# First norms of a two-layer decoder trunk: three due times in a schedule of steps

## The chip, the cores and the metric

The kernel runs on one core of one Trainium2 chip. The metric is the device time of one execution in microseconds (us), and the number that counts is the median over several runs. The engines of the core are called PE (the matrix engine), DVE (the vector engine), ACT (the scalar engine), POOL (GpSimd) and SP (which here issues the DMA transfers).

## The reference

The reference is one inference step of a decoder trunk with two layers, run for a prompt of 1024 tokens and a group of 8 sample tokens, model width 1024. Each layer is an RMS norm, a token mixer (HGRN2 in layer 0, a chunked gated MLP in layer 1), a residual add, and a per-layer embedding that is gated from the residual. Only the beginning matters here: two products that don't depend on each other, the first norm and the first projection.

```python
def rmsnorm(x, g):
    xf = x.astype(jnp.float32)
    y = xf * lax.rsqrt(jnp.mean(xf * xf, axis=-1, keepdims=True) + EPS)
    return (y * g.astype(jnp.float32)).astype(x.dtype)
...
        hn = rmsnorm(h, norm_mix[i])
...
    proj = h @ w_in
...
        h = h + gate * (p[i] @ w_ple_proj[i])
```

## The kernel before

Activations lie with the model width on the partitions (8 tiles of 128, `KT`) and the tokens along the free dimension. The 1032 tokens are cut into three chunks of 384, 384 and 264 columns (`W`, `CH`). Every float32 product is made of three matmuls of a reduced float type (`mm3`, L217 to L221): each operand is split into a high and a low part, and high times high, high times low and low times high are summed in PSUM. So every operand goes through a cast on ACT and a subtraction on DVE or POOL: `split_weights` (L146, L147) for weights, `split` (L214, L215) for activations.

PE's instructions keep the order in which the program issues them. The order on the other engines is chosen when the kernel is compiled, by a scheduler that looks at what is ready, at the program's order and at `high_priority`; on the chip each engine then works through its list strictly in turn. `issue_after(x)` pins what it encloses behind the instruction `x` in the list of x's engine.

The program mixes side work into PE's main stream with a clock of steps, the class `Ticks` (L47). A process (a Python generator) is spawned, and each `yield n` lets it sleep for n steps; `tick()` advances the clock by one and runs what is due, in the order of spawning. A step here is only a place in the program's order, not a time.

The opening is arranged like this. `pple` (L327) makes 12 groups of 6 matmuls, the product of p and half of `w_ple_proj`: 4 groups for chunk 0 (groups 0 to 3), 4 for chunk 1 (4 to 7), 4 for chunk 2 (8 to 11). Each group fills one of three PSUM banks (tag `mm`), which ACT empties (`pple_t`, L338) and SP stores. A `tick()` follows every group. Then come, for each chunk c in turn, `fk(c)` and `qq(c)`, the first two tiles of the projection: 24 matmuls each (`proj`, L298, the same three banks), with one `tick()` in the middle and one at the end. Their weights are the transfers `wstg<-in_wina`; the split of the first is issued during the fill, pinned behind the copy of group 8, and that of the second when `take` fetches the pair ahead of `fk(0)`.

For each chunk a process `first_norm(c)` (L440) runs beside this, with four parts:

- the squares: ACT squares the input tiles `xs` in four instructions (L448), each followed by one add (L449) on DVE for chunk 0 and on POOL for chunks 1 and 2. For chunk 1 the squares are pinned behind the latest `pple_t` copy issued so far, for chunk 2 behind the fourth of the eight casts of a norm (`split4`);
- the sum (`norm_sum`, L257): 24 matmuls of one column against a column of ones (`pss`, L269), then the small add `rms_e` on DVE (L272) and the power -0.5 on POOL (`rsq`, L228), all three with priority;
- the broadcast (`norm_bc`, L275): 6 matmuls that spread `rsq` over the partitions (`pbc`, L280);
- the norm proper, issued with the broadcast: for each of 8 tiles one multiply on DVE (`tmp`, L293), one cast on ACT (`bh`, L214) and one subtraction (`bl`, L215), in turn on POOL and DVE. `fk(c)` and `qq(c)` read `bh` and `bl`.

Where they fall is set by two tables: `SQD` is the step at which a chunk's squares start, and `SDEL[c] = (a, b)` puts the sum a steps behind the squares and the broadcast b steps behind the sum.

```python
SQD = (0, 6, 12)
SDEL = ((6, 3), (6, 2), (4, 2))
...
        yield d[0]
        with tc.high_priority(offset=PRI):
            rs = norm_sum(sp, ssq, c)
        yield d[1]
        pbc = norm_bc(rs, c)
```

Of the kernel before, what the change touches and what calls it, by code (L numbers as in the profile page):

```python
# [31 lines left out]
NWARM = 12  # L32
ZQ = 5
FDEL = ((2, 2), (2, 2), (1, 3))
SQD = (0, 6, 12)
OD = (4, 4)
DL = 4
KB = 1
SDEL = ((6, 3), (6, 2), (4, 2))
NDEL = (((1, 2), (1, 3), (2, 2)), ((2, 2), (2, 4), (3, 3)))  # L40
OFF = (0, 384, 768)
W = (384, 384, 264)
# [38 lines left out]
def trunk_kernel(ctx, tc, xT, st, pT, nrm, wina, lbl, gna, wouta, winb, lng, lnb, lngr, lnbr,  # L81
# [129 lines left out]
    last, rest = {}, {}  # L211

    def split(hi, lo, src, eng=V):
        last["split"] = A.copy(hi, src)  # L214
        last["lo"] = eng.tensor_tensor(lo, src, hi.bitcast(F32), ALU.subtract)  # L215
# [41 lines left out]
    def norm_sum(sp, ssq, c):  # L257

        cols = NT[c] + (c == 2)
        pss = pp.tile([P, 512], F32, name="pss", tag="po", bufs=1)  # L260
        parts = ssq if isinstance(ssq, list) else [ssq]

        if c == 2 and "sq" in rest:
            parts = parts + [rest.pop("sq")]

        for i in range(cols):
            o = min(i * P, W[c] - P)
            for j, t in enumerate(parts):
                PE.matmul(pss[:, i:i + 1], t[:, o:o + P], ones[:, 0:1],  # L269
                          start=j == 0, stop=j == len(parts) - 1)  # L270
        e = sp.tile([P, 3], F32, name="rms_e", bufs=2)
        V.tensor_scalar(e, pss[:, :3], D * EPS, None, ALU.add)  # L272
        return rsqrt(sp, e, 3)

    def norm_bc(y, c):  # L275

        pbc = p2[0].tile([P, 512], F32, name="pbc", tag="p2", bufs=2)
        for i in range(NT[c] + (c == 2)):
            n = min(P, W[c] - i * P)
            PE.matmul(pbc[:, i * P:i * P + n], y[:, i:i + 1].broadcast_to([P, P]), ident[:, P - n:], start=True, stop=True)  # L280
        return pbc

    def norm_proc(sp, ssq, src, gi, hh, hl, c, d):
# [6 lines that stand above are left out]
        w = W[c]  # L290
        for j in range(KT):
            t = sp.tile([P, 384], F32, name="tmp", bufs=4)
            V.scalar_tensor_tensor(t[:, :w], src(j), g32[:, gi, j:j + 1], pbc[:, :w], ALU.mult, ALU.mult)  # L293
            split(hh[:, j, :], hl[:, j, :], t[:, :w], V if j % 2 else G)
            if j == 3:
                last["split4"] = last["split"]

    def proj(wt, xh, xl, c):  # L298

# [140 lines left out]
    def first_norm(c):  # L440
        if c:
            yield SQD[c]
        sq = sp.tile([P, KT, 384], F32, name="sq0", bufs=2)[:, :, :W[c]]
        eng = V if c == 0 else G
        for j in range(0, KT, 2):

            with tc.issue_after(last["pple" if c == 1 else "split4"].ins) if c else ExitStack():
                A.activation(sq[:, j:j + 2, :], xs[c][:, j:j + 2, :], AF.Square)  # L448
            eng.tensor_tensor(sq[:, j, :], sq[:, j, :], sq[:, j + 1, :], ALU.add)  # L449
        yield from norm_proc(sp, [sq[:, j, :] for j in range(0, KT, 2)], lambda j: xs[c][:, j, :], 0, hh[c], hl[c], c, SDEL[c])  # L450

# [34 lines left out]
    for c in CH:  # L486
        tk.spawn(first_norm(c))
# [461 lines left out]
    def norm_spawn(c, ssq, gi, act, d):  # L949
        tk.spawn(norm_proc(sp, ssq[c], lambda j: hr[c][j], gi, act[0][c], act[1][c], c, d[c]))  # L950
# [455 lines left out]
```

## Time and profile before

| | before |
|---|---|
| median of 3 runs | 1919.65 us (1918.82 to 1920.35) |
| the profiled execution's own time | 1921.39 us |
| span of the profile, first to last instruction | 1919.7 us |
| PE busy | 1883.1 us (98% of the span) |
| DVE, ACT, POOL busy | 1156.6, 799.9, 433.4 us |
| mean granted clock of PE | 0.991 of full speed |

The span is what the profiler saw between the first and the last instruction. The time of the same execution is 1.69 us more, for what lies around it, and that execution was 1.74 us slower than the median. A matmul row shows PE busy until a modelled end, so the distance between the starts of neighbouring matmuls tells the pace better than their durations. Where an engine sat idle ahead of an instruction, the row gives the idle time and what ended it in square brackets.

### The profile page before, as it was taken

To read this page: it belongs to the slowest core of one execution; us is meant where nothing else is said; L and a number is where in the kernel's file an instruction comes from. 1 tells how busy PE (TensorE), PEld (TensorE's weight loads), DVE (VectorE), ACT (ScalarE), POOL (GpSimd) and SP (SyncE) were. 2 spreads that over 40 slices of the span, in tenths; PEclk is the share of its full clock that TensorE was granted. 3 is DMA by queue.
4 is the path that set the end of the run, shared out by engine and by line. 5 is a ranking of instruction groups with operands and counts; after the bars stand their busy time and mean duration, and the time that the engine had idled before them with its cause. 6 is when DMAs were issued, how large, how long until landed. Compare 5 with 4: busy or idle time off the path is not lost.

```text
span 1919.7 us, 33670 instructions
## 1 busy us (share of the span) xinstructions
PE 1883.1 (98%) x13250; PEld 1856.4 (97%) x13250; DVE 1156.6 (60%) x2600; ACT 799.9 (42%) x1701; POOL 433.4 (23%) x441
## 2 busy tenths in 40 slices
PE   9999999999999998999999999999999998999997
PEld 8999999999999998999999999999999998999997
DVE  5967676766767676411465755587777766311455
ACT  6453544444454546311244544434434345211342
POOL 4110000000010001011233332344445441011321
PEclk8999999999999999999999999999999998999998
DMA  6232323222231326711243343323323237611123
GB/s 213 75 109 69 116 73 102 78 80 78 92 100 59 111 65 189 256 47 53 73 146 116 109 148 96 93 76 118 125 100 107 100 107 216 197 45 45 67 89 111
DMA packets 123886, 203.75 MB, mean 106 GB/s; under 512 B 11408, under 2 KB 96592, under 8 KB 122704
## 3 DMA queue, kind: packets, MB, share of 16 engines
q1 hardware_dynamic: 123728, 201.61, 32.5%
q8 instruction: 104, 1.70, 0.4%
q14 instruction: 54, 0.44, 0.1%
HBM read 148.75 MB, written 52.82 MB: 105 GB/s over the span
## 4 chain that ended last, share of the span: by engine, by line
PE 90%; DVE 5%; DMA 3%; ACT 1%; issue 1%; POOL 1%; SPq 0%; DVEq 0%; ACTq 0%; POOLq 0%
PE ps_proj L219 18%; PE ps_proj L221 18%; PE ps_proj L220 18%; PE ps_o L219 6%; PE ps_o L220 6%; PE ps_o L221 6%; PE ps_d L221 2%; PE ps_d L219 2%; PE ps_d L220 2%; PE psp L1228 1%; PE pt_o L703 1%; PE pC L658 1%; PE pss L269 1%; PE p L624 1%; DMA vb<-vd 1%
## 5 line engine op out<-in xcount | busy, mean ns | idle before, releaser
L219 PE MATMUL ps_proj<-bh,whi 128*128 128x384 f32 (+1 forms) x2160 | 695.2, 322 | 2.3 <-ACT pple_t L338 1.6
L221 PE MATMUL ps_proj<-bh,wlo 128*128 128x384 f32 (+1 forms) x2160 | 680.0, 315 | 0.6 <-DVE wlo L147 0.5
L220 PE MATMUL ps_proj<-bl,whi 128*128 128x384 f32 (+1 forms) x2160 | 678.9, 314 | 1.2 <-POOL bl L215 1.2
L219 PEld LDWEIGHTS ps_proj<-bh,whi 128*128 128x128 f32 x2160 | 407.5, 189 | 3.8 <-ACT pple_t L338 1.7
L220 PEld LDWEIGHTS ps_proj<-bl,whi 128*128 128x128 f32 x2160 | 407.8, 189 | 2.3 <-POOL bl L215 2.3
L221 PEld LDWEIGHTS ps_proj<-bh,wlo 128*128 128x128 f32 x2160 | 406.6, 188 | 1.8 <-DVE wlo L147 1.8
L147 DVE TENSOR_TENSOR wlo<-wstg,whi 128x1024 fp32r<-128x1024 f32 x148 | 186.2, 1258 | 140.6 <-ACT whi L146 139.8
L146 ACT CAST whi<-wstg 128x1024 fp32r<-128x1024 f32 x148 | 155.1, 1048 | 160.2 <-PE ps_proj L220 105.8
L255 POOL TENSOR_TENSOR ssq<-ssq,tmp 128x384 f32<-128x384 f32 (+1 forms) x72 | 76.1, 1057 | 413.1 <-ACT tmp L254 366.3
L884 DVE TENSOR_TENSOR h<-h,ps_o 128x384 f32<-128x384 f32 (+1 forms) x48 | 24.6, 512 | 193.1 <-PE ps_o L221 192.8
L254 ACT ACTIVATE tmp<-h 128x384 f32<-128x384 f32 (+1 forms) x72 | 35.3, 490 | 219.2 <-DVE h L884 168.9
L219 PE MATMUL ps_o<-bh,whi 128*128 128x384 f32 (+1 forms) x384 | 122.1, 318 | 0.0
L220 PE MATMUL ps_o<-bl,whi 128*128 128x384 f32 (+1 forms) x384 | 121.8, 317 | 0.0
L221 PE MATMUL ps_o<-bh,wlo 128*128 128x384 f32 (+1 forms) x384 | 121.8, 317 | 0.0
L146 ACT CAST shi<-ssum 128x512 fp32r<-128x512 f32 x88 | 54.6, 621 | 109.1 <-PE ps_proj L220 59.2
L219 PE MATMUL ps_o<-zh,whi 128*128 128x384 f32 (+1 forms) x288 | 90.1, 313 | 0.0
L221 PE MATMUL ps_o<-zh,wlo 128*128 128x384 f32 (+1 forms) x288 | 89.8, 312 | 0.0
L220 PE MATMUL ps_o<-zl,whi 128*128 128x384 f32 (+1 forms) x288 | 89.7, 312 | 0.0
L215 POOL TENSOR_TENSOR ql<-q,qh 128x384 fp32r<-128x384 f32 (+1 forms) x24 | 22.3, 928 | 254.0 <-ACT qh L214 254.0
L147 DVE TENSOR_TENSOR slo<-ssum,shi 128x512 fp32r<-128x512 f32 x88 | 68.9, 784 | 11.9 <-ACT shi L146 11.9
L661 DVE TENSOR_TENSOR q<-q,t 128x192 f32<-128x192 f32 (+1 forms) x144 | 47.1, 328 | 45.1 <-PE pC L658 38.7
L220 PEld LDWEIGHTS ps_o<-bl,whi 128*128 128x128 f32 x384 | 72.2, 188 | 0.0
(291 smaller groups left out, 3928.8 us busy)
## 6 DMA issues: line engine op xcount, KB each, us to landing
wstg<-in_wina SPq DMA_DIRECT2D x48, 512.0 KB, 3.7
wstg<-in_winb SPq DMA_DIRECT2D x48, 512.0 KB, 3.9
zstg<-ozd SPq DMA_DIRECT2D x22, 384.0 KB, 4.3
pj<-ppd SPq DMA_DIRECT2D x16, 516.0 KB, 4.5
S<-in_st SPq DMA_DIRECT2D x16, 512.0 KB, 5.4
vb<-vd SPq DMA_DIRECT2D x16, 512.0 KB, 4.4
out_so_s<-S SPq DMA_DIRECT2D x16, 512.0 KB, 3.5
wstg<-in_wouta SPq DMA_DIRECT2D x16, 512.0 KB, 3.5
```

Source lines behind the costliest of these rows:

```text
L146: A.copy(hi, src)
L147: V.tensor_tensor(lo, src, hi.bitcast(F32), ALU.subtract)
L215: last["lo"] = eng.tensor_tensor(lo, src, hi.bitcast(F32), ALU.subtract)
L219: PE.matmul(ps, wh, xh, start=first, stop=False, skip_group_check=more)
L220: PE.matmul(ps, wh, xl, start=False, stop=False, skip_group_check=more)
L221: PE.matmul(ps, wl, xh, start=False, stop=last, skip_group_check=more)
L254: A.activation(sq[:, :w], src, AF.Square)
L255: eng.tensor_tensor(ssq, ssq, sq[:, :w], ALU.add)
L269: PE.matmul(pss[:, i:i + 1], t[:, o:o + P], ones[:, 0:1], start=j == 0, stop=j == len(parts) - 1)
L624: PE.matmul(blk(p0, i), blk(Y, i), blk(X, i), start=True, stop=True)
L661: V.tensor_tensor(ql[:, :, 1, :], ql[:, :, 1, :], t2[:, :, 0:1].broadcast_to([P, n, lv]), ALU.mult)
L884: V.tensor_tensor(hr[c][m], hr[c][m], ps[:, :W[c]], ALU.add)
```

## The change

The steps are worked out from the tables and the order of the ticks; the first tick precedes group 0, so step n is the tick behind group n-2.

| chunk | part | before | after |
|---|---|---|---|
| 0 | sum | behind group 5 | the same |
| 0 | broadcast and norm | behind group 8 | behind group 6 |
| 1 | squares | behind group 5 | behind group 3 |
| 1 | sum | behind group 11 | behind group 9 |
| 1 | broadcast and norm | behind `fk(0)` | behind group 11, ahead of `fk(0)` |
| 2 | squares | behind group 11 | the same |
| 2 | sum | behind `qq(0)` | in the middle of `qq(0)` |
| 2 | broadcast and norm | behind `fk(1)` | in the middle of `fk(1)` |

The squares of chunk 1 stay pinned behind the latest copy, which is now that of group 3 and was that of group 5. As the broadcast of chunk 1 now comes ahead of the squares of chunk 2 in the same step, `split4` is kept for each chunk, and chunk 2's squares stay pinned behind chunk 0's fourth cast.

```diff
-SQD = (0, 6, 12)
+SQD = (0, 4, 12)
-SDEL = ((6, 3), (6, 2), (4, 2))
+SDEL = ((6, 1), (6, 2), (3, 2))
...
             if j == 3:
-                last["split4"] = last["split"]
+                last["split4", c] = last["split"]
...
-            with tc.issue_after(last["pple" if c == 1 else "split4"].ins) if c else ExitStack():
+            with tc.issue_after(last["pple" if c == 1 else ("split4", 0)].ins) if c else ExitStack():
```

## Rows read from the trace of the kernel before

**Rows 1.** The page: busy time, share of the span and instructions of each engine.

```profile
PE 1883.1 (98%) x13250; PEld 1856.4 (97%) x13250; DVE 1156.6 (60%) x2600; ACT 799.9 (42%) x1701; POOL 433.4 (23%) x441
```

**Rows 2.** PE's longest wait from 20 us to the end: total us, times, longest.

```profile
PE ps_pple L219 <- ACT h L338: 8.6, 1, 8.6
```

**Rows 3.** Timeline of PE in the opening: start us, us, what.

```profile
15.12 2.73 PE L269 MATMUL pss<-ones,sq 128*128 128x1 f32 x24
17.71 0.42 PE L219 MATMUL ps_pple<-ph,whi 128*128 128x384 f32 x1
...
21.32 0.41 PE L219 MATMUL ps_pple<-ph,whi 128*128 128x264 f32 x1
...
22.76 0.37 PE L219 MATMUL ps_pple<-ph,whi 128*128 128x264 f32 x1
...
25.04 2.73 PE L269 MATMUL pss<-ones,sq 128*128 128x1 f32 x24
29.38 0.69 PE L219 MATMUL ps_proj<-bh,whi 128*128 128x384 f32 x1 [1.61 <-ACT pple_t L338]
...
36.34 0.83 PE L280 MATMUL pbc<-ident,rsq 128*128 128x128 f32 x6
36.92 0.42 PE L219 MATMUL ps_proj<-bh,whi 128*128 128x384 f32 x1
...
41.20 2.73 PE L269 MATMUL pss<-ones,sq 128*128 128x1 f32 x24
43.79 0.42 PE L219 MATMUL ps_proj<-bh,whi 128*128 128x384 f32 x1
```

**Rows 4.** Stretches of the opening: us, engines' busy us (instructions), granted clock, DMA share, GB/s.

```profile
18.00:22.00 4.00, 4.00 (x17) 4.00 (x16) 0.05 (x1) 1.66 (x4) 2.82 (x3) 0.57 1.07 364
...
30.00:36.00 6.00, 6.00 (x23) 6.00 (x22) 4.74 (x7) 5.45 (x9) 5.21 (x6) 0.56 0.50 155
...
42.00:50.00 8.00, 8.00 (x54) 7.52 (x54) 4.58 (x9) 3.19 (x8) 3.13 (x3) 1.00 0.01 2
```

**Rows 5.** Timeline of ACT in the opening.

```profile
15.69 0.85 ACT L448 ACTIVATE sq<-xs 128x768 f32<-128x768 f32 x1
19.64 0.48 ACT L338 COPY pple_t<-ps_pple 128x384 f32<-128x384 f32 x1 [3.10 <-PE ps_pple L221]
20.01 0.85 ACT L448 ACTIVATE sq<-xs 128x768 f32<-128x768 f32 x1
...
28.53 0.51 ACT L214 CAST bh<-tmp 128x384 fp32r<-128x384 f32 x1 [1.92 <-DVE tmp L293]
28.95 0.93 ACT L338 COPY pple_t<-ps_pple 128x264 f32<-128x264 f32 x3
```

**Rows 6.** Timeline of DVE in the opening.

```profile
27.81 0.16 DVE L272 TENSOR_SCALAR rms_e<-pss 128x3 f32<-128x3 f32 x1 [1.53 <-PE pss L269]
27.89 0.61 DVE L293 SCALAR_TENSOR_TENSOR tmp<-xs,g,pbc 128x384 f32<-128x384 f32 x1
...
33.49 0.75 DVE L215 TENSOR_TENSOR bl<-tmp,bh 128x384 fp32r<-128x384 f32 x1 [0.53 <-ACT bh L214]
34.97 1.67 DVE L147 TENSOR_TENSOR wlo<-wstg,whi 128x1024 fp32r<-128x1024 f32 x1 [0.73 <-ACT whi L146]
```

**Rows 7.** Timeline of POOL in the opening.

```profile
18.13 0.85 POOL L228 TENSOR_TENSOR rsq<-rms_e,mhalf 128x3 f32<-128x3 f32 x1 [17.62 <-DVE rms_e L272]
...
22.86 2.03 POOL L449 TENSOR_TENSOR sq<-sq 128x384 f32<-128x384 f32 x2 [0.92 <-ACT sq L448]
...
33.79 1.77 POOL L449 TENSOR_TENSOR sq<-sq 128x264 f32<-128x264 f32 x2
```

**Rows 8.** The third load of chunk 1's input, issued at 12.26 us: us to landing.

```profile
DMA to landing us min/median/max: 4.8/4.8/4.8
```

**Rows 9.** Groups by line and shape, 8 to 58 us: count, then busy us, mean ns.

```profile
L293 DVE SCALAR_TENSOR_TENSOR tmp<-xs,g,pbc 128x384 f32<-128x384 f32 x16 | 8.9, 606 | 5.6 <-PE pbc L280 5.6
...
L215 DVE TENSOR_TENSOR bl<-tmp,bh 128x384 fp32r<-128x384 f32 x8 | 7.5, 937 | 0.5 <-ACT bh L214 0.5
```

## The prediction

> **What bounds the kernel now.** The page comes first: PE is busy for 98% of the span, every other engine for 60% or less [rows 1], so a saving counts only where it takes away idle time of PE or time that PE spends at half clock. The list of PE's waits comes next: after the opening its longest single wait is 8.6 us, in the fill of the last output phase, which the change doesn't touch [rows 2]. What the change moves lies before 60 us, so I read PE's timeline there, row by row [rows 3], and then the granted clock of the same stretch [rows 4].
>
> Two losses stand in it. Ahead of `fk(0)` PE sits idle for 1.61 us [rows 3]. And twice the clock falls to the lower of its levels, 1.2 instead of 2.4 GHz: the granted clock is 0.57 from 18 to 22 us and 0.56 from 30 to 36 us [rows 4]. The full pace is that of `qq(0)`: 24 matmuls from 36.92 to 41.20 us, 0.178 us each [rows 3]. `fk(0)` has 24 matmuls of the same shape and takes 6.96 us, so the second slow stretch costs 6.96 - 4.28 = 2.68 us. Groups 6 and 7, twelve such matmuls, take 3.61 us instead of 2.14, so the first costs 1.47 us [rows 3]. Each stretch follows a sum of 24 one-column matmuls, which takes 2.59 us (17.71 - 15.12, 43.79 - 41.20) [rows 3].
>
> The timelines of the other engines tell why PE waited. `fk(0)` needs a PSUM bank that ACT has to empty; ACT's copies at 28.95 us stand behind a cast that waited 1.92 us for DVE [rows 5]; and DVE's list had `rms_e` of chunk 1 in front, which waited 1.53 us for the sum to end at about 27.6 us [rows 6]. So a sum with no work behind it that PE could do held up DVE, through DVE ACT, and through ACT PE.
>
> **The change, part by part.** No arithmetic and no transfer is added or removed, and no SP instruction moves in the program; only places in the order change.
>
> *Chunk 0's broadcast, behind group 6 instead of 8.* Group 6 ends halfway through the 3.61 us of groups 6 and 7, at 19.5 us. `rsq` ended at 18.13 + 0.85 = 18.98 us [rows 7], so the broadcast need not wait, unless one of chunk 1's adds stands ahead of it on POOL, 1.0 us each [rows 7]. It costs 0.58 us at either place (36.34 to 36.92 us) [rows 3], and up to twice that at half clock. Chunk 0's multiplies can then begin 2.7 us sooner (it began at 22.76 - 0.58 = 22.18 us).
>
> *Chunk 1's squares, two groups sooner.* They cost nothing new: ACT stood idle for 3.10 us between the first square and the copy of group 6, with the other three squares behind that copy [rows 5]. The inputs must have landed: the third load was issued at 12.26 us and took 4.8 us, so it was there at 17.1 us [rows 8].
>
> *Chunk 1's sum, behind group 9 instead of 11.* A group of chunk 2 takes (25.04 - 22.76) / 3 = 0.76 us [rows 3], so PE reaches the sum at 25.04 - 1.52 = 23.5 us, and the sum ends at 26.1. The adds ended at 22.86 + 2.03 = 24.89 us [rows 7], barely in time before; now they must come 1.4 us sooner. Groups 10 and 11 and the broadcast, 1.52 + 0.58 us, then lie between the sum and `fk(0)`, and cover the chain of DVE and ACT. That is worth the wait, 1.61 us, at most and nothing at least.
>
> *The clock after that sum.* The slow stretch behind it cost 2.68 us. Its row shows a sum and then a gap. In the new order matmuls follow the sum at once, as they did after the first sum, which left a loss of 1.47 us, and after the third, which left none: 42 to 50 us has a granted clock of 1.00 [rows 4]. So the gain is 2.68 - 1.47 = 1.21 us or 2.68. I take 1.21, because the first sum is the one that stands, as this one will, among the groups of the fill. Nothing in the rows excludes a longer slow stretch, which is one of the rivals. Together the two terms give 2.82 to 4.29 us.
>
> A rule of the Trainium skill (TensorE: Matmul & The Clock Gate, section on HAM oscillation) makes PE's idle gaps what sends the clock back to half. By that alone the second stretch would go with its gap and the sum would be 4.29; the row of the first sum, with no gap ahead of the fall, speaks against leaning on it.
>
> *What is late next.* With PE sooner, DVE's chain for chunk 0 may set the pace. Its last subtraction ended at 34.24 us and the low half of the second weights at 36.64 [rows 6]; `qq(0)` uses that in its third matmul, at 36.92 + 0.36 = 37.28 us, so there was 0.64 us to spare. If DVE keeps its order, with `rms_e` ahead of the fifth multiply, the chain moves by 1.52 us with the sum, and `qq(0)` can start at 36.64 - 1.52 - 0.36 = 34.76 us, a gain of 2.16. If the fifth multiply goes ahead of `rms_e`, it can move by up to the 2.7 us of the broadcast, a gain of 3.34. So this caps the gain between 2.16 and 3.34 us. The two bounds meet around 2.8 us, which I take.
>
> *Chunk 2's sum and broadcast, one step sooner.* The adds ended at 33.79 + 1.77 = 35.56 us, and PE came to the sum at 41.20 [rows 3, 7]. It comes half a projection (2.14 us) and the gain sooner, at some 36.3 us, while the adds, pinned behind chunk 0's fourth cast, move forward too. Nothing, while that cover of 0.7 us or more holds; without it PE waits for what is missing, 1 us at the worst.
>
> *Afterwards.* The rows show no resource other than PE with a fixed time behind the opening, so I let the gain carry through whole. It is a difference within the profiled execution (1921.39 us, of which 1919.7 are span); I take it from the median: 1919.65 - 2.8 = **1916.85 us**. What a measurement of this kernel can tell from no change is about 0.2%, 3.84 us; so this forecast counts as the same.
>
> **The rivals.** *The sum waits for its adds.* If ACT's list keeps the remaining squares behind the copies of groups 6 to 8, as now (the second square ran right behind the copy of group 6 [rows 5]), the adds end at 24.9 us or later, PE idles 1.4 us ahead of the sum, and the sum ends at 27.5. Groups 10, 11 and the broadcast bring `fk(0)` to 29.6 us. With a slow stretch of 1.47 to 2.68 us behind it, `qq(0)` starts at 35.4 to 36.6, a gain of 0.3 to 1.5: **1918.7 us** in the middle. For it: the order of ACT is made at compile time, and the loads bound it. Against: the pin is two copies looser.
>
> *The clock stays up.* As after the third sum, no fall: 1.61 + 2.68 = 4.29 us, **1915.4 us**, if DVE's list also changes enough to feed it. For it: the granted clock of 1.00 [rows 4]. Against: the first sum. It is also what the skill's rule on gaps would give.
>
> *The second weights come too late: slower.* Chunk 1's norm is now issued ahead of the fetch of the second weights; before, it was issued behind it. If DVE therefore does chunk 1's steps ahead of `wlo` (L147), `qq(0)` stalls. They cost 8 x 0.606 + 4 x 0.937 = 8.6 us of DVE [rows 9]; all ahead would put the start of `qq(0)` at 34.76 + 8.6 = 43.4 us, 6.4 us later than before: **1926 us**. It decides from 2.2 us of steps ahead, about three multiplies; half of them would give 1921.8. Against: the second weights were split in the gaps of this list before, with DVE idle for 0.73 us ahead of them [rows 6].
>
> **How the numbers follow.** The forecast has 0.43, the clock that stays up 0.25, the sum that waits 0.22, the late weights 0.10. The range goes from 1914.8 (4.29 us and half of the first slow stretch, whose matmuls move against the sum) to 1920.0 (the waiting sum with nothing gained, plus the scatter of the runs); above it lie most of the late weights. Faster by over 0.2% needs 3.84 us: most of the clock that stays up, and a little of the forecast, 0.27. Slower by over 0.2% is the late weights with over half of the steps ahead, 0.05. The rest, 0.68, is the same.
>
> **What would show it.** Right: no wait of PE ahead of `fk(0)`; groups 10 and 11 between the second sum and the broadcast without a gap; `qq(0)` starting near 34 us; a slow stretch of about 3 us behind the second sum. The squares of chunk 1 should run in ACT's former 3.1 us of idle time. Wrong: an idle time ahead of the second `pss` put down to POOL; a wait on `wlo` in `qq(0)`; a slow stretch that still lasts 6 us; or an opening that is 3 us shorter while the end of the kernel comes no sooner.

## The result and the profile after

The changed kernel has a median of 1924.93 us in 8 runs (1922.48 to 1927.84), the kernel before, run beside it on the same chip, 1919.95 us (1918.67 to 1921.51, 8 runs). The ratio is 1.0028 with a 95% interval of 1.0018 to 1.0037: the change makes the kernel 5.4 us slower (3.5 to 7.1). Here and below, what is called slower or faster is worked out from the ratio, not from the two medians (which lie 4.98 us apart). Two runs of the kernel before in the sets below, of 2048.13 and 3747.21 us, are slow ones and are left out of the ratios and means. The forecast was 2.8 us faster, and the measured time lies above its range. The profiled execution took 1927.84 us, the longest of the eight, with a span of 1926.1 us.

Two rows, one from each kernel, measure the opening alike: from the start of chunk 0's sum to the start of `fk(2)`, when all three sums and broadcasts have been issued. Their columns are the length, PE's busy time with its instructions, the granted clock, the DMA share and GB/s. First the kernel before:

```profile
15.12:53.30 38.18, 36.57 (x224) 0.87 0.45 155
```

Then the changed kernel:

```profile
14.68:61.98 47.30, 42.68 (x223) 0.75 0.38 128
```

The opening grew by 9.1 us. Length less busy time is PE's waiting: 1.6 us before, 4.6 after. One less the granted clock, times the length, is about what the lower clock cost: 0.13 x 38.18 = 5.0 us before, 0.25 x 47.30 = 11.8 us after. What is left is the work at full pace, 31.6 and 30.9 us, nearly the same. So, in these two executions, the waits grew by 3.0 us and the cost of the clock by 6.8.

These two executions lie 6.45 us apart (1921.39 and 1927.84), more than the medians, and the opening alone 9.1: behind the start of `fk(2)` the kernel before took 1866.4 us and the changed one 1864.1, for a reason that isn't shown. So the split is theirs and not that of every run. A wider check is on record: the mean granted clock of every execution over its span. One less that clock, times the span, is 19.5 us in the mean of the changed kernel's 8 runs, and 15.6 to 16.5 us in four sets of 29 to 32 runs of the kernel before. So over all runs some 3 to 4 of the 5.4 us, good to about 1 us, are the clock.

Where they lie shows in PE's timeline of the changed kernel (start us, us, what; the counterpart of [rows 3]):

```profile
14.68 2.73 PE L269 MATMUL pss<-ones,sq 128*128 128x1 f32 x24
...
18.60 1.54 PE L280 MATMUL pbc<-ident,rsq 128*128 128x128 f32 x6
...
24.74 3.27 PE L269 MATMUL pss<-ones,sq 128*128 128x1 f32 x18 [0.55 <-POOL sq L449]
30.18 0.59 PE L219 MATMUL ps_pple<-ph,whi 128*128 128x264 f32 x1 [2.17 <-ACT pple_t L338]
...
34.12 0.67 PE L219 MATMUL ps_proj<-bh,whi 128*128 128x384 f32 x1
...
41.53 0.44 PE L221 MATMUL ps_proj<-bh,wlo 128*128 128x384 f32 x1 [1.88 <-DVE wlo L147]
...
44.01 5.11 PE L269 MATMUL pss<-ones,sq 128*128 128x1 f32 x24
48.98 0.67 PE L219 MATMUL ps_proj<-bh,whi 128*128 128x384 f32 x1
```

There is no wait ahead of `fk(0)` any more, at 34.12 us. But group 10 waits 2.17 us for the same thing as `fk(0)` did, a PSUM bank; the third matmul of `qq(0)` waits 1.88 us for the low half of its weights; and chunk 2's sum, now in the middle of `qq(0)`, takes 48.98 - 44.01 = 4.97 us, where it took 2.59 [rows 3]. It ran at the lower of the two levels, 1.2 GHz (stretches of the changed kernel; columns as in [rows 4]):

```profile
40.00:45.00 5.00, 3.47 (x16) 3.47 (x16) 3.24 (x4) 3.37 (x8) 1.41 (x2) 0.76 0.34 105
45.00:53.00 8.00, 8.00 (x33) 8.00 (x33) 0.16 (x1) 0.00 (x0) 0.85 (x1) 0.51 0.01 2
```

The lists of the other two engines tell why. First ACT's timeline in the changed kernel, the counterpart of [rows 5]:

```profile
24.90 0.92 ACT L214 CAST bh<-tmp 128x384 fp32r<-128x384 f32 x2
29.23 0.51 ACT L214 CAST bh<-tmp 128x384 fp32r<-128x384 f32 x1 [3.42 <-DVE tmp L293]
29.65 1.03 ACT L338 COPY pple_t<-ps_pple 128x384 f32<-128x384 f32 x3
...
37.41 1.05 ACT L146 CAST whi<-wstg 128x1024 fp32r<-128x1024 f32 x1
```

The copies of groups 7 to 9 now stand behind seven casts of chunk 0, and the seventh waits 3.42 us for DVE. Then DVE, the counterpart of [rows 6]:

```profile
23.86 0.61 DVE L293 SCALAR_TENSOR_TENSOR tmp<-xs,g,pbc 128x384 f32<-128x384 f32 x1
28.05 0.16 DVE L272 TENSOR_SCALAR rms_e<-pss 128x3 f32<-128x3 f32 x1 [3.58 <-PE pss L269]
...
28.59 0.61 DVE L293 SCALAR_TENSOR_TENSOR tmp<-xs,g,pbc 128x384 f32<-128x384 f32 x1
...
34.56 2.19 DVE L293 SCALAR_TENSOR_TENSOR tmp<-xs,g,pbc 128x384 f32<-128x384 f32 x4 [0.95 <-PE pbc L280]
...
39.20 1.14 DVE L293 SCALAR_TENSOR_TENSOR tmp<-xs,g,pbc 128x384 f32<-128x384 f32 x2 [0.39 <-POOL bl L215]
40.26 1.22 DVE L147 TENSOR_TENSOR wlo<-wstg,whi 128x1024 fp32r<-128x1024 f32 x1
```

`rms_e` of chunk 1 still stands ahead of a multiply of chunk 0, and waits 3.58 us for the sum, so the old chain (sum, DVE, ACT, PSUM bank, PE) is complete; it only ends at group 10. And the split of the second weights comes at 40.26 us, behind all eight multiplies of chunk 1.

### The profile page after: what moved, and what is told of

Its sections match the earlier page's. It is cut to its first block, busy times and chain, and to the rows that moved or that the text cites. A ratio compares the mean times of both kernels' runs of the same rounds, so it can differ in the third digit from the quotient of the medians.

```text
span 1926.1 us, 33671 instructions
## 1 busy us (share of the span) xinstructions
PE 1887.9 (98%) x13250; PEld 1862.3 (97%) x13250; DVE 1160.3 (60%) x2600; ACT 800.1 (42%) x1701; POOL 431.2 (22%) x441
## 4 chain that ended last, share of the span: by engine, by line
PE 90%; DVE 4%; DMA 2%; POOL 1%; ACT 1%; issue 1%; SPq 0%; DVEq 0%; ACTq 0%; POOLq 0%
PE ps_proj L219 18%; PE ps_proj L221 18%; PE ps_proj L220 18%; PE ps_o L219 6%; PE ps_o L220 6%; PE ps_o L221 6%; PE ps_d L221 1%; PE ps_d L219 1%; PE ps_d L220 1%; PE psp L1228 1%; PE pss L269 1%; PE pC L658 1%; PE pt_o L703 1%; PE p L624 1%; PE pt_v L584 1%
## 5 line engine op out<-in xcount | busy, mean ns | idle before, releaser
L147 DVE TENSOR_TENSOR slo<-ssum,shi 128x512 fp32r<-128x512 f32 x88 | 71.5, 813 | 10.6 <-ACT shi L146 10.6
```

What stands on the lines that cost most here:

```text
L147: V.tensor_tensor(lo, src, hi.bitcast(F32), ALU.subtract)
```

## The experiments

Each kernel was timed beside runs of the kernel before on the same chip. "PE waits" and "clock" are of its profiled execution, from the start of chunk 0's sum to that of `fk(2)`, as above. Only one execution of each is profiled, and the clock of single ones scatters: the kernel before has 0.87 in its profile, and two kernels below with the same opening have 0.95 (x_add24) and 0.83 (x_cut32). So the last column gives what the clock cost over the span in the mean of all runs of a kernel, worked out as above and good to about 1 us. The kernel before has 15.6 us beside the kernels p1 to p4, 16.5 beside f1 to f4, 15.7 beside f5 and f6, and 15.9 beside g1 to g4.

| kernel | ratio to before | 95% interval | PE waits us | clock | cost of the clock, all runs, us |
|---|---|---|---|---|---|
| the change | 1.0028 | 1.0018 to 1.0037 | 4.6 | 0.75 | 19.5 |
| p1_broadcast0 | 1.0030 | 1.0018 to 1.0042 | 4.3 | 0.81 | 20.8 |
| p2_chunk1 | 1.0028 | 1.0018 to 1.0038 | 7.5 | 0.92 | 18.8 |
| p3_chunk2 | 0.9998 | 0.9990 to 1.0007 | 2.0 | 0.91 | 16.4 |
| p4_without2 | 1.0023 | 1.0014 to 1.0031 | 5.9 | 0.84 | 17.1 |
| f1_chunk1_weights | 1.0000 | 0.9991 to 1.0009 | 0.4 | 0.76 | 14.2 |
| f2_after_weights | 1.0001 | 0.9993 to 1.0010 | 2.7 | 0.83 | 16.2 |
| f3_after_copies | 1.0050 | 1.0035 to 1.0065 | 7.5 | 0.76 | 22.8 |
| f4_after_both | 1.0009 | 0.9999 to 1.0018 | 2.9 | 0.87 | 16.5 |
| f5_broadcast0_copies | 1.0014 | 1.0005 to 1.0023 | 1.5 | 0.87 | 16.6 |
| f6_all_mended | 1.0008 | 0.9998 to 1.0017 | 1.5 | 0.83 | 16.0 |
| g1_before_wide | 1.0007 | 0.9998 to 1.0016 | 3.7 | 0.91 | 14.8 |
| g2_after_wide | 1.0002 | 0.9993 to 1.0011 | 6.3 | 0.96 | 12.6 |
| g3_after_weights_wide | 0.9985 | 0.9976 to 0.9994 | 3.0 | 1.00 | 12.4 |
| g4_chunk1_weights_wide | 0.9983 | 0.9974 to 0.9992 | 2.6 | 1.00 | 10.6 |

### Which part costs

The change was taken apart: each part alone, and the change without its third part. Each kernel also has the change's two lines for `split4`.

```diff
p1_broadcast0 (against the kernel before)
-SDEL = ((6, 3), (6, 2), (4, 2))
+SDEL = ((6, 1), (6, 2), (4, 2))
p2_chunk1
-SQD = (0, 6, 12)
+SQD = (0, 4, 12)
p3_chunk2
-SDEL = ((6, 3), (6, 2), (4, 2))
+SDEL = ((6, 3), (6, 2), (3, 2))
p4_without2
-SQD = (0, 6, 12)
+SQD = (0, 4, 12)
-SDEL = ((6, 3), (6, 2), (4, 2))
+SDEL = ((6, 1), (6, 2), (4, 2))
```

> Only chunk 0's broadcast two steps sooner. Theory (two lists: ACT's copies stand behind casts that wait for chunk 1's sum, and the second weights' split stands behind chunk 1's norm): no wait on wlo in qq(0), as chunk 1's norm stays behind the fetch; PE may wait for the copies of groups 7 to 9; 1918 to 1921 us. Rival (chunk 2's early sum, run at half clock for 4.97 us, is what costs): no part of it is here, so 1920 us or up to 3 us less.

Measured 1.0030, 5.8 us slower (3.5 to 8.1), more than the theory and the rival had. PE's timeline of this kernel:

```profile
27.44 0.39 PE L219 MATMUL ps_pple<-ph,whi 128*128 128x264 f32 x1 [4.33 <-ACT pple_t L338]
29.80 5.11 PE L269 MATMUL pss<-ones,sq 128*128 128x1 f32 x24
34.77 0.67 PE L219 MATMUL ps_proj<-bh,whi 128*128 128x384 f32 x1
```

There is no wait on `wlo`, as the theory had it, but one of 4.33 us at group 10 for the copies behind the casts, and behind it chunk 1's sum runs at the lower clock, in 34.77 - 29.80 = 4.97 us. The chain ahead of that wait is not the theory's: the sum comes only behind group 11, so no cast ahead of these copies can wait for it. Three copies stand behind seven casts here too, and the seventh multiply waited for POOL, in DVE's list:

```profile
25.85 0.61 DVE L293 SCALAR_TENSOR_TENSOR tmp<-xs,g,pbc 128x384 f32<-128x384 f32 x1 [0.89 <-POOL bl L215]
```

So chunk 0's early broadcast alone costs as much as the whole change.

> Only chunk 1's squares, sum and broadcast two steps sooner. Theory (two lists): a wait of 1.5 to 2 us on wlo in qq(0), as chunk 1's norm is issued ahead of the second weights' fetch; 1921 to 1925 us. Rival (chunk 2's early sum): within 1.5 us of the kernel before.

Measured 1.0028, 5.4 us slower (3.5 to 7.3), with a median of 1924.71 us: in the upper part of the theory's band and against the rival, but with a wait on `wlo` three times as long as the theory's. PE's timeline of this kernel:

```profile
26.95 0.42 PE L219 MATMUL ps_proj<-bh,whi 128*128 128x384 f32 x1
...
39.49 0.69 PE L221 MATMUL ps_proj<-bh,wlo 128*128 128x384 f32 x1 [5.94 <-DVE wlo L147]
```

This part does what it was written for: `fk(0)` starts at 26.95 us with no wait ahead of it, 2.4 us sooner than before [rows 3], of which 0.9 us are an earlier start of its first sum. All of that and more is lost in `qq(0)`, which waits 5.94 us for its weights. DVE's list in this kernel splits them after chunk 1's eighth multiply:

```profile
38.23 1.21 DVE L147 TENSOR_TENSOR wlo<-wstg,whi 128x1024 fp32r<-128x1024 f32 x1
```

> Only chunk 2's sum and broadcast one step sooner. Theory (two lists): within 1 us of the kernel before, the sum stays at 2.6 us because the clock is up where it falls. Rival (chunk 2's early sum): 2 to 5 us slower.

Measured 0.9998 (0.9990 to 1.0007): no change, and the sum takes 2.6 us here. The rival falls: chunk 2's early sum is dear in the changed kernel only because the clock is down when it comes.

> The change without its chunk 2 part. Theory (two lists): as the whole change, 1923 to 1926 us, with a wait of 2 us at group 10 and of 1.5 to 2 us on wlo. Rival (chunk 2's early sum): 1919 to 1921 us.

Measured 1.0023, 4.4 us slower (2.7 to 6.0), with waits of 2.2 us at group 10, 2.4 on `wlo` and 1.4 of the sum for its adds. The first two parts make the loss.

### The two waits taken away

The first mend issues the split of the second weights right behind group 11, ahead of chunk 1's norm (it can't be earlier, since its buffers are those of the fill's weights). The second gives ACT's copies of the fill priority over the casts.

```diff
f1_chunk1_weights (against p2_chunk1), f2_after_weights (against the change)
             with tc.issue_after(last["pple"].ins):
                 load(1)
+        if i == 11:
+            load(2)
         tk.tick()
f3_after_copies (against the change), f5_broadcast0_copies (against p1_broadcast0)
-                with tc.high_priority(offset=PRI if l else 0):
+                with tc.high_priority(offset=PRI if l or half == 0 else 0):
                     last["pple"] = A.copy(t, ps[:, :W[c]])
f4_after_both: both edits
f6_all_mended (against f4_after_both)
-SDEL = ((6, 1), (6, 2), (3, 2))
+SDEL = ((6, 1), (6, 2), (4, 2))
-        eng = V if c == 0 else G
+        eng = V if c < 2 else G
```

> Chunk 1's part alone, with the split of the second weights issued behind group 11, ahead of chunk 1's norm. Theory (two lists): the wait of 5.9 us on wlo in qq(0) goes, and with it what made this part slower; fk(0) still starts near 27 us and qq(0) runs without a long wait: 1915.5 to 1919 us. Rival (DVE simply has too much to do there, and the wait only changes its name): a wait of 3 us or more on bl or tmp in fk(0) or qq(0), 1921 us or more.

> The whole change, with the split of the second weights issued behind group 11. Theory (two lists): the wait of 1.9 us on wlo goes, the wait of 2.2 us at group 10 stays, and chunk 2's sum falls where the clock is up (2.6 us, not 5.0): 1919 to 1922.5 us. Rival: still 1923 us or more.

Measured 1.0000 (0.9991 to 1.0009) and 1.0001 (0.9993 to 1.0010). In both the wait on `wlo` is gone, and with it all of the 5.4 us. So the loss hangs on **the second weights' split behind chunk 1's norm**: without that the other wait, which f2 still has at group 10 (2.17 us), costs nothing against the kernel before; what makes up for it isn't shown. Yet f1, with hardly any wait of PE left in its profile, gains nothing over the kernel before. Its opening, then f2's:

```profile
14.66:56.69 42.03, 41.63 (x223) 0.76 0.42 143
```

```profile
14.43:54.69 40.26, 37.60 (x224) 0.83 0.45 155
```

f1's profile has to be read with care: its execution took 1922.51 us, the longest of 12 with a median of 1918.61. Over all 12 the clock costs 14.2 us, less than the 16.5 of the kernel before beside it.

> The whole change, with priority for ACT's copies of groups 0 to 11. Theory (two lists): the wait of 2.2 us at group 10 goes, as the copies of groups 7 to 9 no longer stand behind the cast that waits for the sum; the wait on wlo stays or grows, to 2 to 5 us: 1921 to 1925 us. Rival (copies are not what holds group 10): the wait at group 10 stays.

Measured 1.0050, 9.6 us slower (6.7 to 12.5), the worst of all and outside the theory's band. The wait at group 10 is gone, as expected, but PE's timeline of this kernel has two others in its place:

```profile
36.13 0.44 PE L219 MATMUL ps_proj<-bh,whi 128*128 128x384 f32 x1 [1.32 <-ACT whi L146]
...
41.72 0.69 PE L221 MATMUL ps_proj<-bh,wlo 128*128 128x384 f32 x1 [4.97 <-DVE wlo L147]
```

With `fk(0)` sooner, PE comes sooner to weights that come no sooner.

> The whole change with both: the copies' priority and the split of the second weights behind group 11. Theory (two lists): both waits go, only the sum's wait of 0.6 us for its adds stays: 1915 to 1919 us, as good as the kernel before or better. Rival: 1921 us or more, with a new wait of 2 us or more in fk(0) or qq(0).

Measured 1.0009 (0.9999 to 1.0018), slightly above the theory's band. What is left are three waits of the sums for POOL's adds, 2.2 us together, and 0.7 on `wlo`.

> Chunk 0's part alone, with priority for ACT's copies of groups 0 to 11. Theory (copies behind casts): the wait of 4.3 us at group 10 goes, and chunk 1's sum falls where the clock is up: 1917 to 1921 us. Rival (the casts' delay comes back): a wait of 2 us or more on bh or bl in fk(0), 1922 us or more.

Measured 1.0014, 2.7 us slower (1.0 to 4.4), in the upper part of the theory's band. The wait at group 10 is gone, and waits of 0.9 on `wlo` and 0.6 on `bl` are there instead. Why it is still slower than the kernel before isn't settled: its profiled execution, 1917.36 us, was the fastest of its 11 runs and shows nothing that would explain it.

> The change without chunk 2's part, with the copies' priority, the second weights' split behind group 11, and chunk 1's adds on DVE. Theory: no wait of PE over 1 us up to qq(2); but because of the cushion no more than 0 to 3 us faster than the kernel before: 1916.5 to 1920 us. Rival (carried whole): 1914 to 1916 us.

Measured 1.0008 (0.9998 to 1.0017). No wait of PE over 0.62 us is left, and nothing is gained. The median, 1919.57 us, is in the theory's band of times, but beside its own runs of the kernel before (1917.76 us) it is 1.5 us slower, not 0 to 3 us faster; and the cushion that the theory gave as the reason isn't there, as x_add24 below shows.

### Is time of the opening carried to the end?

```diff
x_add24 (against the kernel before)
     assert not tk.procs
+    zd = p2[0].tile([P, 512], F32, name="pbc", tag="p2", bufs=2)
+    for _ in range(24):
+        PE.matmul(zd[:, :W[0]], blk(wq[0], 0), hh[0][:, 0, :], start=True, stop=True)
     s0.close()
x_cut32: in proj, for fk(2) and qq(2) of the first head, in place of mm3
+                PE.matmul(ps[:, :W[c]], blk(wh, k), xh[:, k, :], start=k == 0, stop=k == KT - 1)
```

> The kernel before with 24 more matmuls of 384 columns on PE at the end of the opening, behind qq(2): 24 x 0.178 = 4.3 us of PE. Theory (a cushion: behind the opening PE waits for DVE and ACT, so a delay is partly taken up there): the end comes 1.5 to 3.5 us later. Rival (time of the opening is carried whole): 4.0 to 4.6 us later.

Measured 1.0029, 5.6 us slower (3.6 to 7.5). So at least 3.6 us reach the end of the kernel of the 4.3 us that 24 matmuls take at full pace: within the interval the delay is carried whole, and the cushion falls. The opening ahead of it is that of the kernel before, but PE was at the full clock for more of it than there:

```profile
14.68:50.75 36.07, 33.97 (x223) 0.95 0.49 166
```

> The kernel before with the high-low and low-high products left out of fk(2) and qq(2): 32 matmuls of 264 columns less, 32 x 0.121 = 3.9 us of PE at the end of the opening (chunk 2 of q, f and k of the first head is then less exact). Theory (the cushion): DVE and ACT set what follows, so the end comes only 0 to 2 us sooner. Rival (carried whole): 3.5 to 4.2 us sooner.

Measured 0.9992, 1.5 us faster (3.3 faster to 0.2 slower). The theory's band holds it and the rival's doesn't, but in the profile 1.1 us of what was cut comes back right there, as waits of `fk(2)`, `qq(2)` and the next tile on `bh`, `whi` and `wlo`. So this run shows that PE, made faster there, runs into its operands, and not that saved time is lost later. How much of a saving is carried stays open here; g3 and g4 in the next section bear on it.

### What lowers the clock

With the long wait on `wlo` gone, f1, f2, f4 and f6 gained nothing; what their profiles still show is a clock of 0.76 to 0.87. Over all runs the clock costs 14.2 to 16.5 us in them, about as much as in the kernel before or less, so it doesn't explain why f1, with fewer waits, gained nothing; that stays open. But it is time that can still be won. The last edit makes the sums of the first norms 128 columns wide in place of one and reads every 128th column; the waits are left as they are.

```diff
g1 (against the kernel before), g2 (against the change), g3 (against f2_after_weights), g4 (against f1_chunk1_weights)
+        n = P if isinstance(ssq, list) else 1
...
-                PE.matmul(pss[:, i:i + 1], t[:, o:o + P], ones[:, 0:1],
+                PE.matmul(pss[:, i * n:(i + 1) * n], t[:, o:o + P], ones[:, 0:n],
                           start=j == 0, stop=j == len(parts) - 1)
...
-        V.tensor_scalar(e, pss[:, :3], D * EPS, None, ALU.add)
+        V.tensor_scalar(e, pss[:, 0:2 * n + 1:n], D * EPS, None, ALU.add)
```

> The kernel before with the first norms' sums made 128 columns wide instead of one (same result, read from every 128th column): a 128-column broadcast matmul took 0.58 us / 6 = 0.10 us, a one-column sum matmul 2.59 / 24 = 0.11. Theory (the clock falls behind a sum because it moves so few columns): the sums take 2.4 to 3.0 us as before, the granted clock of the opening rises from 0.87 to 0.93 or more: 2 to 4 us faster. Rival (PE's waits are what lowers the clock): no change of the clock, within 1 us.

Measured 1.0007 (0.9998 to 1.0016): nothing was gained. The clock of the profile is 0.91, within the scatter of that opening; over all runs its cost fell by 1.1 us only, from 15.9 to 14.8. PE's waits of this kernel show why, with a new one that the theory had not:

```profile
PE ps_proj L220 <- POOL bl L215: 3.7, 2, 1.9
```

`fk(0)` starts at 25.55 us and outruns chunk 0's norm; the clock is 1.00 up to the first of those waits and falls behind it.

> The whole change with wide sums. Theory (few columns): of the 5.4 us it was slower, the part of the clock goes, 3 to 5 us; the waits at group 10 and on wlo stay: 1919 to 1922.5 us. Rival (PE's waits lower the clock): 1923 us or more.

Measured 1.0002 (0.9993 to 1.0011): the 5.4 us are gone, though PE still waits 6.3 us in this opening, 3.3 of it on `wlo`:

```profile
14.57:55.00 40.43, 34.15 (x224) 0.96 0.45 151
```

The theory holds: over all runs the clock costs 12.6 us in place of 19.5, and the waits alone don't make the kernel slower.

> The change with the second weights' split behind group 11 and wide sums. Theory (few columns): 2 to 5 us faster than the kernel before, and 2 us or more faster than without wide sums. Rival: as without them, within 1 us of the kernel before.

> Chunk 1's part alone with the second weights' split behind group 11 and wide sums. Theory (few columns): 2 to 5 us faster than the kernel before. Rival: as without wide sums, within 1.5 us of the kernel before.

Measured 0.9985 (0.9976 to 0.9994) and 0.9983 (0.9974 to 0.9992): 2.9 and 3.3 us faster than the kernel before, and both intervals lie below 1. The same kernels without wide sums had 1.0001 (f2, against g3) and 1.0000 (f1, against g4); the intervals of each pair meet only at the edge. The two opening rows, g3 first and then g4:

```profile
14.39:49.66 35.27, 32.32 (x223) 1.00 0.50 174
```

```profile
14.71:49.68 34.97, 32.35 (x223) 1.00 0.49 170
```

The clock stays at its full level through the opening, although PE waits 3.0 and 2.6 us in it, most of it at one place in g3's timeline (the sum after that, 24 matmuls at full pace, follows):

```profile
28.81 0.93 PE L281 MATMUL pbc<-ident,rsq 128*128 128x128 f32 x6 [2.50 <-POOL rsq L228]
...
35.86 2.84 PE L270 MATMUL pss<-ones,sq 128*128 128x128 f32 x24
```

Over all runs the clock costs 12.4 us in g3 and 10.6 in g4, 3.8 and 3.6 us less than in f2 and f1, about what was gained over them. And the two openings are 2.9 and 3.2 us shorter than that of the kernel before, the kernels 2.9 and 3.3 us faster: as far as two single profiles can show it, time saved in the opening is kept to the end.

These are the two versions that beat both kernels. Wide sums alone gained nothing (g1), nor did the early steps with early weights (f1, f2); it takes both. Whether early weights and wide sums would do it without the change's early steps wasn't tried.

## Why the prediction was wrong, point by point

- **"Groups 10 and 11 and the broadcast ... cover the chain of DVE and ACT."** This step failed. They stand behind the sum on PE, but they need PSUM banks from the same copies, and those stood behind more of chunk 0's casts than before, because the broadcast had been moved too (p2_chunk1, without that move, has no wait there). `fk(0)` started at 34.12 us, 4.7 us later than before, not 1.6 sooner. The 1.61 us in front of `fk(0)` became 2.17 us in front of group 10, and 4.33 us in p1_broadcast0, where only that broadcast moved. The prediction weighed the broadcast by the multiplies that it sets free, and not by the copies that its casts overtake on ACT.
- **The late weights.** Place and mechanism of this rival were right, and it had been given 0.10. The reason against it, that DVE had 0.73 us of idle time ahead of that split, was a reading of a list made for another order. In the changed kernel all eight multiplies of chunk 1 stand ahead, PE waits 1.88 us, and 5.94 us where little else holds PE up (p2_chunk1). f2_after_weights takes this alone away, and with it the 5.4 us, while f3_after_copies, which takes away the wait at group 10 alone, is 9.6 us slower. So of the two steps this one decides the time.
- **The clock: a gain of 1.21 us.** It was a loss of 6.8 us in the profiled execution, and of 3 to 4 over all runs. The term had bounds of 1.21 and 2.68 us of gain, with a longer slow stretch named among the rivals and priced in none. What was missed is that a sum that falls where the clock is down takes 4.97 us in place of 2.59, and that PE is at the lower clock behind both of the long new waits (a granted clock of 0.50 from 30 to 34 us and from 44 to 52; ahead of the first it was down already, 0.50 from 26 to 28). The term was also taken from one execution: the first slow stretch, 1.47 us, doesn't come in x_add24, which has the same opening and a granted clock of 1.00 from 12 to 26 us.
- **The Trainium skill's rule** (TensorE: Matmul & The Clock Gate, section on HAM oscillation), by which long idle gaps of PE bring the clock down, was applied to a gap of 1.61 us and weighed down by the first sum's row. The runs bear the doubt out in part: the profiled execution of f1_chunk1_weights has 0.4 us of gaps and a clock of 0.76. But gaps matter too: g1_before_wide has wide sums, gaps of 3.7 us and 0.91, and in p2_chunk1 the clock fell during the wait of 5.94 us.
- **The sum that waits for its adds** came too, at 0.55 us instead of 1.4, and as it was described: ACT kept the other three squares behind the copy of group 6:

```profile
18.62 0.48 ACT L338 COPY pple_t<-ps_pple 128x384 f32<-128x384 f32 x1 [2.51 <-PE ps_pple L221]
18.99 0.85 ACT L448 ACTIVATE sq<-xs 128x768 f32<-128x768 f32 x1
```

- **What is late next** was capped at a gain of 2.16 to 3.34 us by DVE's chain. The only kernels that gain anything gain 2.9 and 3.3 us. That the numbers lie close is chance as far as is shown: those kernels also split the second weights sooner and have wide sums, and neither is in the prediction.
- **"I let the gain carry through whole."** For a delay this holds within the interval (x_add24); for a gain, g3 and g4 agree with it.
- **The range.** Its lower end, 1914.8, is 0.2 us above the sum given for it (1919.65 - 4.29 - 0.73 = 1914.6). Nothing hangs on it.

## What to carry to other kernels

When work is moved forward on an engine whose list is made at compile time, ask what now stands behind it in the lists of the other engines: here a bank's copies and the next weights' split, both further down the program and both needed sooner than the work that overtook them. Time a part of a schedule change alone before adding the parts up, since two parts that cost 5.8 and 5.4 us alone cost 5.4 together. And where PE's clock falls around a run of one-column matmuls, try the same matmuls with more columns beside the move: here neither gained anything alone.

## What was not expected of the hardware

A matmul of one column took as long as one of 128: 24 sums have 2.59 us from start to start of what follows at the full clock, and the profile gives a row of 24 one-column matmuls 2.73 us and one of 24 wide ones 2.84 us. From start to start the wide sums of g3 take 2.59 to 2.60 us too. Each of these matmuls loads 128 by 128 squares as its weights, whatever its columns. At the lower clock the one-column sum took 4.97 us, nearly twice.

With wide sums in place of one-column ones, the granted clock of the opening went from 0.83 to 1.00 (f2 to g3) and from 0.76 to 1.00 (f1 to g4), with more waiting of PE and not less (2.7 to 3.0 and 0.4 to 2.6 us). Over all runs the clock's cost fell with it by 3.8 and 3.6 us, and by 6.9 from the change to g2. Behind none of the twelve wide sums in the profiles of g1 to g4 did the clock fall before PE had waited. Not every one-column sum is followed by a fall either: in p2_chunk1 the granted clock is 1.00 from 14 to 36 us, with two of them in it, and 1.00 from 44 to 57 us, with the third.
